# Attention in steps of two blocks, gates over the whole array, and another order in the last stripe of a hybrid decoder step

## The chip, the core and the metric

The kernel runs on one core of a Trainium2 chip. A core has a matrix engine (TensorE, PE in the profile, with its weight loads as PEld), a vector engine (VectorE, DVE), an engine for activation functions (ScalarE, ACT), a general engine (GpSimd, POOL) and an engine that here only issues DMAs (SyncE, SP). Each works through its own queue in order, and semaphores tie them together. Matmuls write to PSUM, eight banks of 512 floats in each of 128 partitions; everything else lies in SBUF. The metric is the device time of one execution in microseconds (us), lower is better.

## What is computed

One layer of a hybrid decoder: 1024 prompt tokens and 8 sample tokens, one after the other branch, in fp32. The parts that the change touches are the gates of the recurrence (16 blocks of 64 channels, two 64x64 matrices each), the blocked attention (3 groups of 8 heads, 8 query blocks of 128, each against one or two key blocks) and the output projection with its norm:

```python
def rg_lru(xc, h0, w_a, b_a, w_x, b_x, lam):
    xb = xc.reshape(B, T, N_RNN_BLOCKS, RNN_BLOCK)
    r = sigmoid(einsum('btnc,ncd->btnd', xb, w_a) + b_a)
    i = sigmoid(einsum('btnc,ncd->btnd', xb, w_x) + b_x)
    ...
def dilated_attention_prompt(q, k, v, window, dilation, slopes):
    ...
    s = jnp.where(mask, einsum('brnqhe,brnkhe->brnhqk', qb, kc) * HEAD_DIM ** -0.5 + bias, NEG_INF)
    lse = logsumexp(s, axis=-1)
    o = einsum('brnhqk,brnkhe->brnqhe', exp(s - lse[..., None]), vc)
def hybrid_layer(...):
    proj = rms_norm(x, norm_pre) @ w_in
    u, z_rnn, q, k, v, z_attn, g_rnn, g_attn = split(proj)
    ...
    mixed = sigmoid(g_rnn) * y_rnn + sigmoid(g_attn) * y_attn
    return x + rms_norm(mixed @ w_out, norm_post)
```

## The kernel before

**Products.** Every large product is made of three fp32r products, since operands are split into a high and a low part (`xh`, `xl`; `whi`, `wlo`): high x high, high x low, low x high, all accumulated in one PSUM tile with the tag `pj`. `project` makes a 128-column matrix in three chunks of tokens (256, 384 and 392 wide, 24 matmuls each); an `evac` on ACT or DVE then takes the chunk out of PSUM. There are 3 `pj` tiles, 3 `s` tiles, 1 `pt` and 1 `o`: all eight banks.

**Order.** All code is recorded in the order in which it is written, and each engine keeps that order. The projections run one after another: `u` and `z` of the recurrence, `za`, six gate matrices `g`, then for each of four head pairs `hp` and three groups `g` the matrices v, k and q, then the other `g`. Everything else is in generators on lanes ("lru", "attention", "merge", "sample"). After every half chunk (12 matmuls) `tick` lets each lane that is due make one step; what a generator yields is how many planned nanoseconds of PE work later its next step is due. When the arena of SBUF slots (`NSLOT` of them) is empty, `Arena.get` calls `force`, which runs the next due lane steps at once, with no projection work between them, until a slot is free.

**Gates.** `chain(j)` takes the channel blocks 2j and 2j+1 through convolution, gates and scan; `chain_front` holds the gate products. For each half `s` of 64 channels and each chunk, the high weights `lh` multiply the tile `xs[s]` (its one half of the partitions holds the high part of the input, the other half the low part) over all 128 rows, and the low weights `ll` multiply the 64 rows with the high part only. The result goes to an `s` tile, from which two sigmoids on ACT (L591) take it. All three chunks are one lane step.

**Attention.** `attention(g, hp)` has 12 steps. Step b does `turn(b - 2)` (transposes of the probabilities into `pt`, copied to `PT`), `scores(b)` (one matmul per head, 64 rows each, into an `s` tile of its own; a fused add and minimum on DVE, L802; the exponential on ACT, L806), and `values(b - 4)` (64 output columns per head, four blocks in one `o` tile). Steps also hold `v_rows` and `k_rows`, which transpose v and k.

**Last stripe.** The output projection is made in four stripes of 256 columns; in each, blocks 0 to 7 of the prompt and then block 8 (the 8 sample rows) are multiplied (`out_block`). In the last stripe `finish` closes blocks in groups, after blocks 2, 4, 6 and 8: reciprocal root on DVE and ACT, scale and residual, store. For blocks in `SHARED` one half of the columns goes through ACT and POOL.

Of the kernel before, what the change touches and what calls it, by code (L numbers as in the profile page):

```python
# [29 lines left out]
NSLOT = 43  # L30
# [3 lines left out]
LAG, STEP = 2, 1700  # L34
# [35 lines left out]
def hybrid_step(ctx: ExitStack, tc: tile.TileContext, I, O):  # L70
# [10 lines left out]
    def ps_tile(tag):  # L81
        bufs = {"pj": 3, "s": 3, "pt": 1, "o": 1}[tag]
        return psum.tile([128, 512], F32, tag=tag, bufs=bufs, name="ps_" + tag)
# [468 lines left out]

    def chain_front(b, X, R, T):
# [27 lines left out]
        for s in range(2):  # L581
            rows = slice(64 * s, 64 * s + 64)
            ws = slice(128 * s, 128 * s + 128)
            for c0, n in CHUNKS:
                p = ps_tile("s")
                cs = slice(c0, c0 + n)
                mm(p[:, :n], lh[:, ws], xs[s][:, cs], start=True, stop=False)
                mm(p[:, :n], ll[rows, ws], xs[s][rows, cs], start=False, stop=True)
                for gate in range(2):
                    at = 64 * (gate ^ s)  # L590
                    nc.scalar.activation(G[gate][rows, cs], p[at:at + 64, :n], AF.Sigmoid,  # L591
                                         bias=par[rows, b, 5 + gate:6 + gate])
            yield 1500
# [184 lines left out]
    def attention(g, hp):  # L778
# [14 lines left out]
        def scores(b):  # L793
            k0, n = keys(b)
            pt = P[b] = small.tile([128, 2, 256], F32, tag="P", name="P", bufs=LAG + 1)
            base = C["base2"] if g == 2 else C["base0"][:, 256 - 128 * n:256]
            for h in range(2):
                p = ps_tile("s")
                hs = slice(64 * h, 64 * h + 64)
                mm(p[:, :128 * n], qt[hs, 128 * b:128 * b + 128], kt[hs, 128 * k0:128 * (k0 + n)],  # L800
                                 start=True, stop=True)
                nc.vector.tensor_tensor_reduce(out=pt[:, h, :128 * n], in0=p[:, :128 * n], in1=base,  # L802
                                               scale=-SLOPES[g][2 * hp + h] * DIL[g], scalar=3e38,
                                               op0=OP.add, op1=OP.min, accum_out=st[:, g, 0, h, b:b + 1])
            for h in range(2):
                nc.scalar.activation(pt[:, h, :128 * n], pt[:, h, :128 * n], AF.Exp, scale=-1.0,  # L806
                                     bias=st[:, g, 0, h, b:b + 1], accum_out=st[:, g, 1, h, b:b + 1])

        def turn(b):
            k0, n = keys(b)  # L810
            pt = P.pop(b)
            p = ps_tile("pt")
            for h in range(2):
                for kb in range(n):
                    tr(p[:, (h * n + kb) * 128:(h * n + kb) * 128 + 128],
                                        pt[:, h, 128 * kb:128 * kb + 128], ident)
            t = PT[b] = small.tile([128, 2 * n, 128], F32, tag="PT", name="PT", bufs=LAG + 1)
            src = p[:, :256 * n].rearrange("p (b c) -> p b c", c=128)
            if b % 2:
                nc.vector.tensor_copy(t, src)  # L820
            else:
                nc.scalar.activation(t, src, AF.Copy)

        def values(b):
            k0, n = keys(b)
            vn = vns[g, hp]
            t = PT.pop(b)
            if b % 4 == 0:
                PO[0] = ps_tile("o")
            o = PO[0]  # L830
            off = 128 * (b % 4)
            for kb in range(n):
                for h in range(2):
                    mm(o[64 * h:64 * h + 64, off:off + 128], vn[:, k0 + kb, 64 * h:64 * h + 64],
                                     t[:, h * n + kb], start=kb == 0, stop=kb == n - 1)
            if b % 4 == 3:
                f = b // 4
# [10 lines left out]
        for b in range(8 + 2 * LAG):  # L848
            if LAG <= b < 8 + LAG:
                turn(b - LAG)  # L850
            if b < 8:
                scores(b)
            if b >= 2 * LAG:
                values(b - 2 * LAG)
            if b < 2:
                v_rows(g, hp, b)
            elif 6 <= b < 8:
                k_rows(g, hp, b - 6)
            if b == 7:
                ar.free(kts.pop((g, hp)), qts.pop((g, hp)))  # L860
            if b == 7 + 2 * LAG:
# [304 lines left out]
    for e in started:  # L1166
        advance(e)
    C = late_consts()
# [122 lines left out]
    SHARED = (5, 6, 7)  # L1291
    ends = {2: (0, 1, 2), 4: (3, 4), 6: (5, 6), 8: (7, 8)}

    def finish(tbs):
# [4 lines left out]
        for q, tb in enumerate(tbs):  # L1299
# [3 lines left out]
            own = slice(0, 512 if tb in SHARED else D)  # L1303
            nc.vector.scalar_tensor_tensor(o[:m, own], o[:m, own], r[:m, q:q + 1], x[:m, own], op0=OP.mult, op1=OP.add)
            nc.sync.dma_start(dst[:, own], o[:m, own])
# [41 lines left out]
    order = range(9)  # L1347
    for s in range(4):
        wts = [W.use(), W.use(2)]
# [38 lines left out]
```

## Time and profile before

| | before |
|---|---|
| median of three runs | 1315.66 us (1314.17 to 1316.99) |
| the profiled execution, its own time | 1316.49 us |
| its span, first to last instruction | 1314.1 us |
| PE busy | 1294.3 us (98%) |
| PEld busy | 1203.1 us (92%) |
| DVE busy | 604.8 us (46%) |
| ACT busy | 550.0 us (42%) |
| POOL busy | 219.8 us (17%) |
| PE's share of the chain that ended last | 94% |

How to read it: a group of the table of lines gives busy time, count and mean duration, but matmuls are pipelined, so a matmul's duration says little about its cost. What a matmul costs PE is the distance from its start to the start of the next one, and that is read from the timeline. The timeline gives start, duration, engine, line, operation, tiles and shapes; `64*128` is rows times columns of the loaded weights, `x4` means that four instructions of one kind were merged into one row. An fp32 matmul (scores, values) leaves two records, an fp32r matmul and a transpose one.

### The profile page before, as it was taken

The page shows a single profiled execution, that of the slowest core. Times are in us where ns is not written, and L with a number is a line of the kernel's source. Part 1 is how long each engine was busy: PE and PEld are TensorE (multiplying, and loading weights), DVE is VectorE, ACT ScalarE, POOL GpSimd, SP SyncE. Part 2 cuts the span into 40 slices and gives each one's busy share as a digit, 9 for nine tenths or more (in the row PEclk, how much of TensorE's full clock was granted, in tenths as well). Part 3 has the DMA queues.
Part 4 walks back from the last instruction along what each step waited for, and adds up shares of the span by engine and source line. Part 5 has one row for each costly group of instructions (what it writes and reads, how often), then busy time and mean ns, then how long its engine had stood idle before and what let it go on. Part 6 is the DMA issues. An engine that isn't in the chain of part 4 may idle for free.

```text
span 1314.1 us, 21425 instructions
## 1 busy us (share of the span) xinstructions
PE 1294.3 (98%) x8726; PEld 1203.1 (92%) x8726; DVE 604.8 (46%) x1300; ACT 550.0 (42%) x1223; POOL 219.8 (17%) x228
## 2 busy tenths in 40 slices
PE   8999999999999999999999999999999999999996
PEld 8998999989998898888988988888989999999996
DVE  6552744827436324533345325544244245555225
ACT  6548357384574343334334333333563222122222
POOL 4001402314022002240016002140026000001001
PEclk9999999999999999999999999999999999999998
DMA  7201300423302017312354115421285356313033
GB/s 237 69 23 33 98 16 17 145 81 131 95 17 89 25 41 206 87 51 65 89 137 102 41 41 169 109 66 45 50 228 158 120 184 211 105 65 98 32 113 146
DMA packets 149303, 125.96 MB, mean 96 GB/s; under 512 B 8857, under 2 KB 135289, under 8 KB 149198
## 3 DMA queue, kind: packets, MB, share of 16 engines
q1 hardware_dynamic: 149206, 124.61, 31.6%
q8 instruction: 68, 1.11, 0.4%
q14 instruction: 29, 0.24, 0.1%
HBM read 98.44 MB, written 26.21 MB: 95 GB/s over the span
## 4 chain that ended last, share of the span: by engine, by line
PE 94%; DVE 2%; ACT 1%; issue 1%; DMA 0%; POOLq 0%; POOL 0%; SPq 0%; ACTq 0%; DVEq 0%
PE ps_pj L146 79%; PE ps_s L146 7%; PE ps_o L146 3%; PE ps_s L150 3%; PE ps_pt L150 2%; DVE ck L1036 1%; ACT P L806 0%; DMA wraw<-in_w_in 0%; DVE wlo L226 0%; DVE tanh L631 0%; ACT whi L225 0%; DVE PT L820 0%; DVE P L802 0%; POOLq L1384 0%; ACT whi L243 0%
## 5 line engine op out<-in xcount | busy, mean ns | idle before, releaser
L146 PE MATMUL ps_pj<-xh,whi 128*128 128x256 f32 (+3 forms) x1760 | 579.1, 329 | 0.0
L146 PE MATMUL ps_pj<-xh,wlo 128*128 128x256 f32 (+3 forms) x1760 | 558.1, 317 | 0.3 <-DVE wlo L239 0.3
L146 PE MATMUL ps_pj<-xl,whi 128*128 128x256 f32 (+3 forms) x1760 | 558.0, 317 | 0.0
L146 PEld LDWEIGHTS ps_pj<-xh,whi 128*128 128x128 f32 x1760 | 331.6, 188 | 22.8 <-issue 20.9
L146 PEld LDWEIGHTS ps_pj<-xl,whi 128*128 128x128 f32 x1760 | 331.8, 189 | 0.2
L146 PEld LDWEIGHTS ps_pj<-xh,wlo 128*128 128x128 f32 x1760 | 331.4, 188 | 0.5 <-DVE wlo L239 0.5
L226 DVE TENSOR_TENSOR wlo<-wraw,whi 128x512 fp32r<-128x512 f32 x176 | 152.5, 867 | 296.3 <-ACT whi L225 285.9
L806 ACT ACTIVATE P<-P,stat 128x128 f32<-128x128 f32 (+1 forms) x192 | 85.0, 443 | 123.9 <-DVE stat L802 123.8
L225 ACT ACTIVATE whi<-wraw 128x512 fp32r<-128x512 f32 x176 | 109.4, 623 | 7.6 <-DVE tanh L632 3.0
L146 PE MATMUL ps_pj<-wlo,mh 128*128 128x256 f32 (+1 forms) x288 | 79.1, 281 | 0.0
L146 PE MATMUL ps_pj<-whi,ml 128*128 128x256 f32 x256 | 72.0, 281 | 0.0
L146 PE MATMUL ps_pj<-whi,mh 128*128 128x256 f32 x256 | 72.0, 281 | 0.0
L802 DVE CUSTOM_DVE_ANT_0 P<-ps_s,base 128x128 f32<-128x128 f32 (+1 forms) x192 | 59.7, 347 | 21.6 <-PE ps_s L146 18.2
L820 DVE COPY PT<-ps_pt 128x512 f32<-128x512 f32 (+1 forms) x48 | 28.8, 600 | 87.8 <-PE ps_pt L150 49.9
L706 ACT ACTIVATE qt<-ps_pj,qsc 128x384 f32<-128x384 f32 (+1 forms) x36 | 27.4, 762 | 94.8 <-PE ps_pj L146 94.8
L146 PE MATMUL ps_s<-kt,qt 64*128 64x128 f32 (+1 forms) x384 | 59.0, 372 | 3.2 <-DVE stat L802 3.2
L146 PE MATMUL ps_pj<-hzl,whi 128*128 128x256 f32 (+2 forms) x192 | 61.5, 320 | 0.0
L146 PE MATMUL ps_pj<-hzh,wlo 128*128 128x256 f32 (+2 forms) x192 | 61.5, 320 | 0.0
L146 PE MATMUL ps_pj<-hzh,whi 128*128 128x256 f32 (+2 forms) x192 | 61.4, 320 | 0.0
L1088 ACT ACTIVATE sg<-ps_pj 128x256 f32<-128x256 f32 (+2 forms) x48 | 21.9, 457 | 92.8 <-PE ps_pj L146 90.8
L591 ACT ACTIVATE gate<-ps_s,par 64x256 f32<-64x256 f32 (+2 forms) x96 | 52.1, 542 | 13.2 <-PE ps_s L146 10.5
L146 PE MATMUL ps_o<-PT,vn 128*64 128x128 f32 x560 | 52.2, 292 | 1.3 <-ACT ot L846 1.3
(243 smaller groups left out, 1679.2 us busy)
## 6 DMA issues: line engine op xcount, KB each, us to landing
wraw<-in_w_in SPq DMA_DIRECT2D x72, 512.0 KB
ck<-in_cache_kv_w SPq DMA_DIRECT2D x24, 512.0 KB
sgd<-sg SPq DMA_DIRECT2D x16, 516.0 KB
sgl<-sgd SPq DMA_DIRECT2D x16, 516.0 KB
xin<-in_x_prompt SPq DMA_DIRECT2D x16, 512.0 KB
qb<-sd SPq DMA_DIRECT2D x12, 512.0 KB
fb<-fd SPq DMA_DIRECT2D x24, 256.0 KB
hzd<-uc SPq DMA_DIRECT2D x8, 516.0 KB
```

The source lines that it names most:

```text
L146: nc.tensor.matmul(out, lhsT, rhs, start=start, stop=stop)
L150: nc.tensor.transpose(out, in_, idn)
L225: nc.scalar.activation(hi[:, a:b], raw[:, a:b], AF.Copy)
L226: nc.vector.tensor_tensor(lo[:, a:b], raw[:, a:b], f32(hi[:, a:b]), op=OP.subtract)
L591: nc.scalar.activation(G[gate][rows, cs], p[at:at + 64, :n], AF.Sigmoid, bias=par[rows, b, 5 + gate:6 + gate])
L706: nc.scalar.activation(dst, src, AF.Copy, scale=C["qsc"][:, g, hp:hp + 1])
L802: nc.vector.tensor_tensor_reduce(out=pt[:, h, :128 * n], in0=p[:, :128 * n], in1=base, scale=-SLOPES[g][2 * hp + h] * DIL[g], scalar=3e38, ...
L806: nc.scalar.activation(pt[:, h, :128 * n], pt[:, h, :128 * n], AF.Exp, scale=-1.0, bias=st[:, g, 0, h, b:b + 1], accum_out=st[:, g, 1, h, ...
L820: nc.vector.tensor_copy(t, src)
L1036: nc.vector.tensor_tensor(acc, acc, t, op=OP.add)
L1088: nc.scalar.activation(z[:, c0:c0 + n], p[:, :n], AF.Sigmoid)
```

## The change

Five edits, none of which changes what is computed.

1. PSUM: `pj` goes from 3 tiles to 2, `pt` from 1 to 2. The arena loses one slot.
2. Gates: the low weights lie in two fixed tiles `low_w` of which the quarters that must not count are zero (cleared once on POOL), so that the second product also runs over all 128 rows. Only the two quarters that matter are subtracted on DVE. The lane now yields after every chunk, 1300 planned ns, in place of after three chunks, 1500.
3. Attention: a step takes two blocks. `turn`, `scores` and `values` get a pair; there are 6 steps, due 3400 planned ns apart in place of 1700. The scores of one head of both blocks share one `s` tile.
4. Last stripe: the sample rows (block 8) come first, block 7 last; `finish` runs after 8, 1, 3, 5, 6 and 7.
5. `SHARED` is now 4, 5, 6; block 7 is finished in two column halves on DVE, each stored as soon as it is done.

```diff
-NSLOT = 43
+NSLOT = 42
-LAG, STEP = 2, 1700
+STEP = 3400
...
-        bufs = {"pj": 3, "s": 3, "pt": 1, "o": 1}[tag]
+        bufs = {"pj": 2, "s": 3, "pt": 2, "o": 1}[tag]
...
+    low_w = [const.tile([128, 256], F32R, name=f"low_w{i}") for i in range(2)]
+
+    def clear_low_w():
+        for t in low_w:
+            for q in range(2):
+                nc.gpsimd.tensor_scalar(t[:, 128 * q:128 * q + 128], ident, 0.0, None, op0=OP.mult)
...
-        ll = small.tile([128, 256], F32R, tag="t2", name="ll")
+        ll = low_w[b % 2]
         nc.scalar.activation(lh, lw, AF.Copy)
-        nc.vector.tensor_tensor(ll, lw, f32(lh), op=OP.subtract)
+        for s in range(2):
+            rows, ws = slice(64 * s, 64 * s + 64), slice(128 * s, 128 * s + 128)
+            nc.vector.tensor_tensor(ll[rows, ws], lw[rows, ws], f32(lh[rows, ws]), op=OP.subtract)
...
                 mm(p[:, :n], lh[:, ws], xs[s][:, cs], start=True, stop=False)
-                mm(p[:, :n], ll[rows, ws], xs[s][rows, cs], start=False, stop=True)
+                mm(p[:, :n], ll[:, ws], xs[s][:, cs], start=False, stop=True)
...
-            yield 1500
+                yield 1300
...
+        def scores(bs):
+
+            ps = [ps_tile("s") for _ in range(2)]
+            for b in bs:
+                k0, n = keys(b)
+                off = 256 * (b % 2)
+                for h in range(2):
+                    hs = slice(64 * h, 64 * h + 64)
+                    mm(ps[h][:, off:off + 128 * n], qt[hs, 128 * b:128 * b + 128], kt[hs, 128 * k0:128 * (k0 + n)],
+                       start=True, stop=True)
...
-        for b in range(8 + 2 * LAG):
-            if LAG <= b < 8 + LAG:
-                turn(b - LAG)
-            if b < 8:
-                scores(b)
-            if b >= 2 * LAG:
-                values(b - 2 * LAG)
...
+        pairs = [(2 * i, 2 * i + 1) for i in range(4)]
+        for i in range(6):
+            if 1 <= i < 5:
+                turn(pairs[i - 1])
+            if i < 4:
+                scores(pairs[i])
+            if i >= 2:
+                values(pairs[i - 2])
+            if i < 2:
+                v_rows(g, hp, i)
+            elif i < 4:
+                k_rows(g, hp, i - 2)
...
-    SHARED = (5, 6, 7)
-    ends = {2: (0, 1, 2), 4: (3, 4), 6: (5, 6), 8: (7, 8)}
+    SHARED = (4, 5, 6)
+    ends = {8: (8,), 1: (0, 1), 3: (2, 3), 5: (4, 5), 6: (6,), 7: (7,)}
...
+            parts = [slice(0, 512)] if tb in SHARED else [slice(0, 512), slice(512, D)] if tb == 7 else [slice(0, D)]
...
-    order = range(9)
     for s in range(4):
+
+        order = list(range(9)) if s < 3 else [8] + list(range(8))
```

Three places show how the instructions stand. The first is PE's queue at a gate step of channel blocks 2 and 3. Before, one step holds three chunks (`uc` is the tile `xs[s]`):

```order
L146 MATMUL ps_pj<-xh_20_119,wlo_1942 128x392
L146 MATMUL ps_s<-uc_118_2018,lh 128x256
L146 MATMUL ps_s<-uc_118_2018,ll 128x256
L146 MATMUL ps_s<-uc_118_2018,lh 128x384
L146 MATMUL ps_s<-uc_118_2018,ll 128x384
L146 MATMUL ps_s<-uc_118_2018,lh 128x392
L146 MATMUL ps_s<-uc_118_2018,ll 128x392
L146 MATMUL ps_pj<-xh_21_120,whi_1941 128x392
```

Now most chunks stand alone between half chunks of a projection, but the last eight of these two channel blocks stand in a row, between the last chunk of `z` of block 7 and the first of `za` (the next free slot of the arena was wanted there):

```order
L146 MATMUL ps_pj<-xh_24_123,wlo_2125 128x392
L146 MATMUL ps_s<-uc_120_2090,lh 128x392
L146 MATMUL ps_s<-uc_120_2090,low_w_135 128x392
L146 MATMUL ps_s<-uc_125_2174,lh 128x392
L146 MATMUL ps_s<-uc_125_2174,low_w_136 128x392
L146 MATMUL ps_s<-uc_121_2091,lh 128x256
L146 MATMUL ps_s<-uc_121_2091,low_w_135 128x256
L146 MATMUL ps_s<-uc_126_2175,lh 128x256
L146 MATMUL ps_s<-uc_126_2175,low_w_136 128x256
L146 MATMUL ps_s<-uc_121_2091,lh 128x384
L146 MATMUL ps_s<-uc_121_2091,low_w_135 128x384
L146 MATMUL ps_s<-uc_126_2175,lh 128x384
```

What moved: six matmuls of one step became six steps of two, except for this run of sixteen (twelve rows shown are its beginning), which no projection work divides.

The second place is PE's queue in the attention of head pair 1, group 0. Before, two steps of one block each, with twelve projection matmuls between them:

```order
L146 MATMUL ps_pj<-xh_24_123,wlo_5227 128x256
L150 MATMUL ps_pt<-ident,P 128x128 x4
L146 MATMUL ps_s<-kt_4919,qt_5095 128x256 x2
L146 MATMUL ps_o<-PT,vn_5264 64x128 x4
...
L146 MATMUL ps_pj<-xh_20_119,wlo_5227 128x384
L150 MATMUL ps_pt<-ident,P 128x128 x4
L146 MATMUL ps_s<-kt_4919,qt_5095 128x256 x2
L146 MATMUL ps_o<-PT,vn_5264 64x128 x4
```

Now one step of two blocks:

```order
L146 MATMUL ps_pj<-xl_28_127,whi_5216 128x384
L146 MATMUL ps_pj<-xh_20_119,wlo_5217 128x384
L150 MATMUL ps_pt<-ident,P 128x128 x8
L146 MATMUL ps_s<-kt_4926,qt_5075 128x256 x4
L146 MATMUL ps_o<-PT,vn_5253 64x128 x8
L146 MATMUL ps_pj<-xh_21_120,whi_5216 128x384
```

What moved: the instructions are the same, but transposes, scores and values of two blocks stand together, and 24 or 36 projection matmuls stand between two steps.

The third place is ACT's queue in the first attention call (head pair 0, group 0). Before, all gates of blocks 6 and 7 stood ahead of it, and one table load preceded its exponentials:

```order
L617 ACTIVATE sq_3773<-tanh_3692 128x1032
L706 ACTIVATE qt_3723<-ps_pj,qsc 128x384 x2
L708 ACTIVATE smp<-ps_pj 128x8
L225 ACTIVATE whi_3818<-wraw_3600 128x512
L806 ACT_TABLE_LOAD
L806 ACTIVATE P,stat<-P,stat 128x128 x2
```

Now the sigmoids of those gates stand between the exponentials, each change with a table load:

```order
L823 ACT_TABLE_LOAD
L823 ACTIVATE P,stat<-P,stat 128x128 x2
L823 ACTIVATE P,stat<-P,stat 128x256 x2
L601 ACT_TABLE_LOAD
L601 ACTIVATE gate_3803<-ps_s,par 64x256
L601 ACTIVATE gate_3804<-ps_s,par 64x256
L225 ACTIVATE whi_3746<-wraw_3542 128x512
L601 ACTIVATE gate_3825<-ps_s,par 64x256
L601 ACTIVATE gate_3826<-ps_s,par 64x256
L840 ACTIVATE PT<-ps_pt 128x256
L823 ACT_TABLE_LOAD
L823 ACTIVATE P,stat<-P,stat 128x256 x4
```

What moved: the last part of the recurrence (blocks 6 and 7) now runs beside the first attention calls; ACT's queue has 37 table loads where it had 31.

## Rows read from the trace of the kernel before

**Rows 1.** The page's table of engines: busy us (share of the span) and instructions.
```profile
PE 1294.3 (98%) x8726; PEld 1203.1 (92%) x8726; DVE 604.8 (46%) x1300; ACT 550.0 (42%) x1223; POOL 219.8 (17%) x228
```

**Rows 2.** Timeline of PE around one gate step: start us, duration us, engine, line, tiles.
```profile
186.37 0.34 PE L146 MATMUL ps_pj<-xh,wlo 128*128 128x384 f32 x1
186.55 0.28 PE L146 MATMUL ps_s<-uc,lh 128*128 128x256 f32 x1
186.76 0.38 PE L146 MATMUL ps_s<-uc,ll 64*128 64x256 f32 x1
187.07 0.44 PE L146 MATMUL ps_s<-uc,lh 128*128 128x384 f32 x1
...
188.54 0.44 PE L146 MATMUL ps_pj<-xh,whi 128*128 128x392 f32 x1
188.83 0.34 PE L146 MATMUL ps_pj<-xl,whi 128*128 128x392 f32 x1
189.01 0.34 PE L146 MATMUL ps_pj<-xh,wlo 128*128 128x392 f32 x1
```

**Rows 3.** Table of PE's groups by shape: count, busy us, mean ns.
```profile
L146 PE MATMUL ps_s<-uc,lh 128*128 128x256 f32 x16 | 4.5, 279 | 0.0
```

**Rows 4.** Timeline of PE in the attention of head pair 0, group 1.
```profile
552.43 0.44 PE L146 MATMUL ps_o<-PT,vn 128*64 128x128 f32 x4
552.80 0.39 PE L146 MATMUL ps_pj<-xh,whi 128*128 128x256 f32 x1
...
555.63 0.28 PE L146 MATMUL ps_pj<-xh,wlo 128*128 128x256 f32 x1
555.75 0.60 PE L150 MATMUL ps_pt<-ident,P 128*128 128x128 f32 x4
556.28 0.70 PE L146 MATMUL ps_s<-kt,qt 64*128 64x256 f32 x4
556.91 0.66 PE L146 MATMUL ps_o<-PT,vn 128*64 128x128 f32 x8
557.50 0.44 PE L146 MATMUL ps_pj<-xh,whi 128*128 128x384 f32 x1
557.78 0.34 PE L146 MATMUL ps_pj<-xl,whi 128*128 128x384 f32 x1
```

**Rows 5.** Timeline of PE as a chunk of the third za matrix starts.
```profile
251.65 0.34 PE L146 MATMUL ps_pj<-xh,whi 128*128 128x392 f32 x1
```

**Rows 6.** Timeline of ACT: first half of the evacuation of the chunk two before it.
```profile
252.74 0.36 ACT L676 ACTIVATE za<-ps_pj 128x256 f32<-128x256 f32 x1
```

**Rows 7.** Timeline of DVE: the second half of that evacuation.
```profile
255.46 0.42 DVE L677 TENSOR_TENSOR za<-ps_pj,za 128x256 f32<-128x256 f32 x1
```

**Rows 8.** Timeline of ACT: the six sigmoids of one gate step.
```profile
200.64 3.31 ACT L591 ACTIVATE gate<-ps_s,par 64x256 f32<-64x256 f32 x6
```

**Rows 9.** Waits of PE: us in total, times, longest us.
```profile
PE ps_s L146 <- DVE stat L802: 3.2, 3, 1.9
PE ps_o L146 <- ACT ot L846: 1.3, 1, 1.3
PE ps_pt L150 <- DVE PT L820: 1.2, 1, 1.2
```

**Rows 10.** Stretches: length, busy us of PE, PEld, DVE, ACT, POOL, PE clock, DMA.
```profile
864.00:866.00 2.00, 0.53 (x3) 0.49 (x4) 2.00 (x7) 0.49 (x2) 1.94 (x1) 0.99 0.00 0
866.00:869.40 3.40, 3.40 (x16) 2.42 (x15) 2.46 (x6) 2.67 (x10) 3.32 (x2) 0.50 0.38 108
```

**Rows 11.** The page's groups: exponentials and table loads on ACT in attention.
```profile
L806 ACT ACTIVATE P<-P,stat 128x128 f32<-128x128 f32 (+1 forms) x192 | 85.0, 443 | 123.9 <-DVE stat L802 123.8
...
L806 ACT ACT_TABLE_LOAD x6 | 7.7, 1283 | 2.7 <-DVE stat L802 2.6
```

**Rows 12.** Timeline of all engines at the end of the span.
```profile
1303.80 0.28 PE L146 MATMUL ps_pj<-whi,mhl 128*72 128x256 f32 x1
...
1305.92 0.14 DVE L1297 TENSOR_REDUCE sst<-ssq 128x2 f32<-128x8 f32 x1
...
1307.53 1.94 DVE L1304 SCALAR_TENSOR_TENSOR on<-on,rstd,xin 128x512 f32<-128x512 f32 x2
...
1311.04 0.30 SPq L1305 DMA_DIRECT2D out_y_s<-on  x1
```

More of the change, by code (lines that the diff above doesn't have):

```diff
@@ L791, in keys @@
             return (b, 1)
[L793 to L813, printed above, removed]
-                for kb in range(n):
[L815 to L837, printed above, removed]
+        def scores(bs):
[7 more added lines that the diff above has]
+                       start=True, stop=True)
+            for b in bs:
+                k0, n = keys(b)
+                off = 256 * (b % 2)
+                pt = P[b] = small.tile([128, 2, 256], F32, tag="P", name="P", bufs=2)
+                base = C["base2"] if g == 2 else C["base0"][:, 256 - 128 * n:256]
+                for h in range(2):
+                    nc.vector.tensor_tensor_reduce(out=pt[:, h, :128 * n], in0=ps[h][:, off:off + 128 * n], in1=base,
+                                                   scale=-SLOPES[g][2 * hp + h] * DIL[g], scalar=3e38,
+                                                   op0=OP.add, op1=OP.min, accum_out=st[:, g, 0, h, b:b + 1])
+                for h in range(2):
+                    nc.scalar.activation(pt[:, h, :128 * n], pt[:, h, :128 * n], AF.Exp, scale=-1.0,
+                                         bias=st[:, g, 0, h, b:b + 1], accum_out=st[:, g, 1, h, b:b + 1])
@@ new lines, in turn @@
+        def turn(bs):
+            for b in bs:
+                k0, n = keys(b)
+                pt = P.pop(b)
+                p = ps_tile("pt")
+                for h in range(2):
+                    for kb in range(n):
+                        tr(p[:, (h * n + kb) * 128:(h * n + kb) * 128 + 128],
+                           pt[:, h, 128 * kb:128 * kb + 128], ident)
+                t = PT[b] = small.tile([128, 2 * n, 128], F32, tag="PT", name="PT", bufs=4)
+                src = p[:, :256 * n].rearrange("p (b c) -> p b c", c=128)
+                if b % 2:
+                    nc.vector.tensor_copy(t, src)
+                else:
+                    nc.scalar.activation(t, src, AF.Copy)
@@ new lines, in values @@
+        def values(bs):
+            vn = vns[g, hp]
+            for b in bs:
+                k0, n = keys(b)
+                t = PT.pop(b)
+                if b % 4 == 0:
+                    PO[0] = ps_tile("o")
+                o = PO[0]
+                off = 128 * (b % 4)
+                for kb in range(n):
+                    for h in range(2):
+                        mm(o[64 * h:64 * h + 64, off:off + 128], vn[:, k0 + kb, 64 * h:64 * h + 64],
+                           t[:, h * n + kb], start=kb == 0, stop=kb == n - 1)
+            if bs[-1] % 4 == 3:
+                f = bs[-1] // 4
+                o = PO[0]
@@ L846, in values @@
                 nc.scalar.activation(dst, src, AF.Copy)
-        for b in range(8 + 2 * LAG):
-            if LAG <= b < 8 + LAG:
-                turn(b - LAG)
-            if b < 8:
-                scores(b)
-            if b >= 2 * LAG:
-                values(b - 2 * LAG)
[L855 to L859, printed above, removed]
+        pairs = [(2 * i, 2 * i + 1) for i in range(4)]
[10 more added lines that the diff above has]
+                k_rows(g, hp, i - 2)
+            if i == 3:
                 ar.free(kts.pop((g, hp)), qts.pop((g, hp)))
-            if b == 7 + 2 * LAG:
+            if i == 5:
                 ar.free(vns.pop((g, hp)))
@@ L1167, in hybrid_step @@
         advance(e)
+    clear_low_w()
     C = late_consts()
@@ L1302, in finish @@
             dst = O["y_p"][0, tb * 128:(tb + 1) * 128] if tb < 8 else O["y_s"].rearrange("b o d -> (b o) d")
-            own = slice(0, 512 if tb in SHARED else D)
-            nc.vector.scalar_tensor_tensor(o[:m, own], o[:m, own], r[:m, q:q + 1], x[:m, own], op0=OP.mult, op1=OP.add)
-            nc.sync.dma_start(dst[:, own], o[:m, own])
+            parts = [slice(0, 512)] if tb in SHARED else [slice(0, 512), slice(512, D)] if tb == 7 else [slice(0, D)]
+            for own in parts:
+                nc.vector.scalar_tensor_tensor(o[:m, own], o[:m, own], r[:m, q:q + 1], x[:m, own],
+                                               op0=OP.mult, op1=OP.add)
+                nc.sync.dma_start(dst[:, own], o[:m, own])
             if tb in SHARED:
```

## The prediction

> **What bounds the kernel now.** I read the table of engines first: PE is busy in 98% of the span, DVE in 46%, ACT in 42% [rows 1]. So time is gained only where PE's queue gets shorter or stops waiting, and lost only where it waits. But a busy PE isn't a PE at its pace. I therefore went on to PE's timeline and took distances from start to start. Inside a projection a 256-column matmul costs 0.12 us (555.63 to 555.75 [rows 4]), a 384-column one 0.18 us (186.37 to 186.55), a 392-column one 0.18 us (188.83 to 189.01 [rows 2]). Where PE goes from 128-row weights to 64 rows or 64 columns, or back, it costs more, and the whole change is about the number of such places. Then I read the waits of PE: those in attention make 5.7 us [rows 9], so there is little waiting left to take away. Last I read when PSUM tiles come free, since edit 1 takes one from the projections.
>
> **Gates over the whole array.** In the gate step of rows 2 the 256-column product with 128 rows (`lh`) starts at 186.55 and the 64-row one (`ll`) at 186.76, 0.21 us in place of 0.12; `ll` lasts to 187.07, 0.31 us in place of 0.12. From 186.55 to 188.83, when the first projection matmul behind the step is through, it is 2.28 us. At the projection's pace the same seven matmuls are 2 x (0.12 + 0.18 + 0.18) + 0.18 = 1.14 us. With zeros in the unused quarters all of them are 128x128 fp32r matmuls like those of the projection, so I take the whole difference, 1.14 us, and there are 16 such steps [rows 3]: **-18.2 us**. That the chunks now stand alone costs nothing by this price, as no shape changes. DVE subtracts a quarter as many elements in two instructions; the cover is DVE's idle half.
>
> A rule of the Trainium skill speaks against this edit: "TensorE: Matmul & The Clock Gate", section "Why this matters for your kernels", says a matmul with few rows takes as long as one with all of them, and gains only from running beside others. By it full rows would give nothing here, and the sum would be 18.2 us higher. The row differs: `ll` took 0.31 us where a 256-column matmul takes 0.12 [rows 2, 4].
>
> **Attention in pairs.** A full step (transposes, scores, values) runs from 555.75 to 557.50, 1.75 us, and the first projection matmul behind it takes 0.28 us (557.50 to 557.78), 0.10 more than usual. In a pair, what does the second block save? The way into the 64-row shape: 0.09 us (0.21 less 0.12 in rows 2). The way back: 0.10 us. Of the values: two matmuls (four records) took 0.37 us (552.43 to 552.80), four took 0.59 us (556.91 to 557.50) [rows 4]; so a matmul is 0.11 us and 0.15 us is the way in and out. For scores and transposes I take no gain, each passes at its price. Twelve steps become six: the two merges without values save 0.09 + 0.10 = 0.19 us each, the four with values 0.34 us. That is 1.74 us a call, and 12 calls make **-20.9 us**. Bounds: 0.10 us a merge (only the way back), 7 us in all, to 25 us if the scores' second pair also overlaps. I stay at 20.9, since each part is a row.
>
> **The end.** PE's last matmul starts at 1303.80 and is through at 1304.08; the span ends 10.0 us later [rows 1, 12], and the last store is issued at 1311.04, 7.0 us behind PE, held up in SP's queue by the half block that went through ACT and POOL. Now block 7 is last and is finished on DVE alone. By the same rows, shifted, ACT is first at block 6's scaling till about 0.6 us behind PE (an estimate); square and product take 0.9 us more; from the reduce to the scaling it is 1.61 us (1305.92 to 1307.53); two halves of 512 columns take 1.4 us (1.94 us for one of 512 and one of 1024 columns, so 0.7 for 512). The last store is issued some 4.6 us behind PE: 2.4 us earlier, but it is a larger one. **-2.1 us** (-1.5 to -2.6). Between ends the groups of at most two blocks keep DVE free in time for two PSUM tiles.
>
> **Waits that go.** Scores waited for `s` tiles (3.2 us), values for `o` (1.3), transposes for the single `pt` (1.2) [rows 9]; pairs with 24 matmuls between them and a second `pt` tile give each more time. Behind the longest one (PE busy 0.53 of 2.00 us) the clock was granted at 0.50, that is 1.2 GHz, for 3.40 us, in which 16 matmuls passed [rows 10]; that costs half, 1.7 us. Of 7.4 us in all I count half gone, since DVE's long sample instructions stay: **-3.7 us** (0 to -7.4).
>
> **Two `pj` tiles.** The chunk that starts at 251.65 [rows 5] would now need the tile whose evacuation ACT does at 252.74 [rows 6] and DVE ends at 255.46 + 0.42 = 255.88 [rows 7]: 4.2 us late. DVE and ACT are then in the recurrence's burst of long instructions, which runs at its own pace, so PE, once it has waited, is behind that burst and doesn't wait the same time again. I take 4.2 us once and 0.5 us for smaller cases: **+4.7 us** (1, if the burst falls elsewhere, to 9, if it happens at two of them).
>
> **Sixteen gate matmuls in a row.** At the end of `z` of block 7, eight chunks now stand in PE's queue with three `s` tiles. Each needs two sigmoids, 3.31 / 6 = 0.55 us each [rows 8]. The eighth chunk starts when the sigmoids of the fifth are done: 0.3 + 10 x 0.55 + 0.36 to its end = 6.2 us, against 2.6 us of PE work. **+3.5 us** (2 to 6, the latter if all 8.8 us of ACT show).
>
> **The recurrence beside the first attention.** The gates of blocks 6 and 7 now fall between the exponentials of the first call: six more table loads, 1283 ns each [rows 11], 7.7 us of ACT in some 25 us. In a step ACT then has four exponentials (4 x 0.44), two loads (2.6) and two to four sigmoids (1.1 to 2.2), 5.5 to 6.6 us, against a period of about 24 x 0.18 + 3 = 7.3 us of PE. It fits narrowly: **+2 us** (0 to 8). Small excursions of sample and merge that now stand alone: **+0.5 us**. Clearing `low_w` on POOL, one slot less: nothing, weight pieces stand in the same order on ACT.
>
> **Sum.** -18.2 - 20.9 - 2.1 - 3.7 + 4.7 + 3.5 + 2 + 0.5 = -34.2 us. The profiled execution took 1316.49 us, which gives 1282.3; it lies 0.8 us over the median of 1315.66, so the forecast is **1281.5 us**.
>
> **The rivals.** (a) The 64-row matmul isn't slow for its shape but for its operands (`xs` is rewritten just before); then full rows give nothing: 1281.5 + 18.2 = 1299.7. For it: the `lh` products between them are slow as well (187.07 onward). Against it: the first `lh`, on the same operands, takes the usual 279 ns [rows 3] and the step to `ll` starts the loss. Chance 0.07.
> (b) The clock. In the run of sixteen and in the waits for `pj` PE is busy less than half of the time, as it was before the 3.40 us at 1.2 GHz [rows 10]. Three such falls at 1.7 us, and 3 us more of waiting for ACT: 1281.5 + 8 = 1289.5. Chance 0.15. The Trainium skill has this: "TensorE: Matmul & The Clock Gate", section "A second HAM failure mode: psum-queue depth-cycling", says that short PE pauses at PSUM tiles bring the clock down again and again. By it each such place here pays 1.7 us more; rows 9 show three waits of over 1 us, and rows 10 a fall behind one.
> (c) Slower: a turn now needs the four exponentials of the step just before, not of two steps before. Four reduces and four exponentials end about 2.5 us behind the scores; the cover is 24 matmuls and the values, some 5 us. If ACT and DVE have over 2.5 us of other work queued ahead of them in every step, PE waits in all 48 turns (4 in each of 12 calls). It decides at 34.2 / 48 = 0.7 us a turn; at 1 us the time is 1281.5 + 48 = 1329.5. Against it: ACT is busy 42%, and its own idle time ahead of exponentials, 123.9 us, is waiting for DVE's result [rows 11], not work. Chance 0.03.
> (d) The order shows that pairs and full rows are really there; that an edit does nothing can be left out for these.
>
> **How the numbers follow.** The forecast has 0.75, (a) 0.07, (b) 0.15, (c) 0.03. The forecast's own range from its terms, not all at their ends together, is 1271 to 1293; (b) lies inside it. (a) and (c), 0.10, are left out above, and about 0.08 of the rest on both sides. So 1271 to 1295. A measurement of this kernel can tell 0.2% (2.6 us) from no change. All cases but (c) are faster: 0.96 faster, 0.01 same, 0.03 slower.
>
> **What would show it.** In the profile after: the distance from `lh` to `low_w` and from `low_w` onward at 0.12 to 0.18 us; 72 attention steps, a full pair near 3.2 us; waits of PE for `pj` behind ACT or DVE between 200 and 260 us; a stretch of some 6 us with eight gate chunks; the last store some 4.6 us behind PE. It is wrong if PE's own distances don't shrink, or if waits at turns and tiles sum to over 20 us.

## The result and the profile after

The changed kernel takes 1293.1 us (median; 1290.8 to 1295.5), against 1315.3 us before: ratio 0.983, 95% interval 0.981 to 0.985. That is 22.2 us faster; the forecast was 34.2. The time lies within the range, 1.9 us below its upper end, nearer to the 1289.5 of rival (b) than to the forecast. The profiled execution took 1294.3 us with a span of 1292.5.

The page's table of engines after, to be held against [rows 1], and the view of cores (span, mean granted clock):

```profile
PE 1258.5 (97%) x8726; PEld 1209.8 (94%) x8726; DVE 604.6 (47%) x1323; ACT 553.2 (43%) x1231; POOL 221.9 (17%) x232
```
```profile
core 0: 1292.5 us, clock 0.987
```

PE's busy time fell by 36 us, the span by 22 only. So PE now has 34 us without work where it had 20, and its mean clock is 0.987 where the profile before has 0.996. **The work shrank more than forecast, and much of that was given back as waits and as clock.** First the work. Timeline of PE after, around one gate chunk:

```profile
103.93 0.28 PE L146 MATMUL ps_s<-uc,lh 128*128 128x256 f32 x1
104.05 0.28 PE L146 MATMUL ps_s<-uc,low_w 128*128 128x256 f32 x1
104.17 0.34 PE L146 MATMUL ps_pj<-xh,whi 128*128 128x392 f32 x1
```

From start to start, `lh` and `low_w` cost 0.12 us each, where [rows 2] had 0.21 and 0.31. And a full pair in group 0 (transposes, scores, values, then the first projection matmuls behind them):

```profile
559.70 1.03 PE L150 MATMUL ps_pt<-ident,P 128*128 128x128 f32 x8
560.66 1.14 PE L146 MATMUL ps_s<-kt,qt 64*128 64x256 f32 x8
561.73 1.09 PE L146 MATMUL ps_o<-PT,vn 128*64 128x128 f32 x16
562.75 0.44 PE L146 MATMUL ps_pj<-xh,whi 128*128 128x384 f32 x1
563.03 0.34 PE L146 MATMUL ps_pj<-xl,whi 128*128 128x384 f32 x1
```

Against two of the steps of [rows 4] (0.53 + 0.63 + 0.59, and 0.10 on the way back): transposes 0.96 for 1.06, scores 1.07 for 1.26, values 1.02 for 1.18, one way back for two. That is 0.55 us a pair. Over the 12 calls, added up from start to start and with the transposes of v and k that stand there, attention's places cost about 136 us of PE in place of 168.

Now what came back. Waits of PE after (us in total, times, longest):

```profile
PE ps_pj L146 <- DVE za L687: 11.0, 5, 4.9
PE ps_s L146 <- ACT gate L601: 2.7, 5, 0.7
PE ps_pj L146 <- ACT whi L225: 2.7, 1, 2.7
PE ps_pt L150 <- ACT P L823: 2.3, 2, 2.2
```

The three waits of [rows 9] are gone; these four took their place, 18.7 us for 5.7. And the clock: stretches of the kernel after (length, busy us of PE, PEld, DVE, ACT, POOL, PE clock, DMA share, GB/s):

```profile
11.80:15.20 3.40, 3.01 (x14) 3.02 (x15) 2.08 (x5) 1.64 (x5) 2.83 (x8) 0.51 1.11 375
220.00:223.40 3.40, 3.40 (x18) 3.40 (x17) 0.00 (x0) 3.27 (x6) 1.78 (x1) 0.50 0.00 0
243.90:250.70 6.80, 3.88 (x12) 3.88 (x13) 6.70 (x5) 0.00 (x0) 2.79 (x2) 0.50 0.00 0
264.30:267.70 3.40, 3.35 (x10) 3.35 (x11) 3.32 (x6) 0.00 (x0) 0.00 (x0) 0.51 0.35 103
458.90:462.30 3.40, 3.40 (x23) 2.57 (x20) 1.79 (x10) 2.36 (x9) 2.31 (x1) 0.50 0.02 5
...
1182.50:1189.30 6.80, 6.30 (x28) 6.01 (x29) 2.41 (x4) 1.82 (x5) 0.00 (x0) 0.50 0.90 303
sum 30.60, PE 26.74 PEld 25.57 DVE 17.36 ACT 9.10 POOL 9.72; mean PE 3.82 PEld 3.65 DVE 2.48 ACT 1.30 POOL 1.39
```

PE worked 26.7 us at 1.2 GHz (clock 0.50); half of it, 13 us, would not be there at 2.4 GHz. Before there was one such stretch ahead of PE's end [rows 10], 1.7 us. The first of the seven, 1.5 us of the 13, lies in the kernel's start; the profile of e10, whose start is that of the kernel before, has one there too (12.1 to 15.5 us), so it isn't to be put down to the change. Ahead of most of the others stands one of the waits, with PE busy for 0.1 to 0.6 of the time:

```profile
213.00:220.00 7.00, 4.32 (x21) 2.95 (x20) 0.57 (x1) 6.57 (x13) 0.00 (x0) 1.00 0.26 75
261.00:264.30 3.30, 0.52 (x3) 0.20 (x2) 2.97 (x4) 2.89 (x6) 0.00 (x0) 1.00 0.80 320
1180.00:1182.50 2.50, 0.20 (x2) 0.00 (x0) 0.57 (x1) 0.86 (x2) 0.74 (x3) 1.00 0.69 213
```

### The profile page after: what moved, and what is told of

Read it like the earlier page. It is cut to its first block, busy times and chain, and to the rows that moved or that the text cites. A ratio compares the mean times of both kernels' runs of the same rounds, so it can differ in the third digit from the quotient of the medians.

```text
span 1292.5 us, 21498 instructions
## 1 busy us (share of the span) xinstructions
PE 1258.5 (97%) x8726; PEld 1209.8 (94%) x8726; DVE 604.6 (47%) x1323; ACT 553.2 (43%) x1231; POOL 221.9 (17%) x232
## 4 chain that ended last, share of the span: by engine, by line
PE 87%; ACT 5%; DVE 5%; issue 1%; DMA 1%; POOL 0%; SPq 0%; DVEq 0%; ACTq 0%
PE ps_pj L146 75%; PE ps_s L146 5%; PE ps_o L146 3%; PE ps_s L150 3%; PE ps_pt L150 2%; ACT gate L601 1%; DVE wlo L226 1%; DVE tanh L641 1%; ACT whi L225 1%; DMA wraw<-in_w_in 1%; DVE ck L1057 1%; ACT gate L623 1%; ACT sq L627 0%; ACT P L823 0%; ACT L627 0%
## 5 line engine op out<-in xcount | busy, mean ns | idle before, releaser
L146 PE MATMUL ps_pj<-xh,whi 128*128 128x256 f32 (+3 forms) x1760 | 574.7, 327 | 12.1 <-DVE za L687 11.0
L146 PEld LDWEIGHTS ps_pj<-xh,whi 128*128 128x128 f32 x1760 | 334.0, 190 | 21.0 <-DVE za L687 12.4
L226 DVE TENSOR_TENSOR wlo<-wraw,whi 128x512 fp32r<-128x512 f32 x176 | 149.6, 852 | 320.0 <-ACT whi L225 314.0
L819 DVE CUSTOM_DVE_ANT_0 P<-ps_s,base 128x128 f32<-128x128 f32 (+1 forms) x192 | 56.0, 348 | 8.5 <-PE ps_s L146 8.0
L840 ACT ACTIVATE PT<-ps_pt 128x256 f32<-128x256 f32 (+1 forms) x48 | 21.0, 437 | 91.0 <-PE ps_pt L150 90.9
L146 PEld LDWEIGHTS ps_pj<-wlo,mh 128*128 128x128 f32 (+1 forms) x288 | 52.3, 181 | 0.5 <-DVE wlo L226 0.4
```

Source lines behind the costliest of these rows:

```text
L146: nc.tensor.matmul(out, lhsT, rhs, start=start, stop=stop)
L226: nc.vector.tensor_tensor(lo[:, a:b], raw[:, a:b], f32(hi[:, a:b]), op=OP.subtract)
```

## Experiments

**Theory.** Pairs and full rows are worth what PE's distances say (32 and 18.8 us); what is missing comes back by four side effects of the change: two `pj` tiles, the gates cut into single chunks ("the cut" from here on), one slot fewer, and the clock behind the waits. **Rivals.** One of the two large edits gives less than its distances; the `za` waits come from one side effect alone; the late weights have nothing to do with the slot.

The diffs are against the kernel before (e1 to e4, e10, e12) or after (e5 to e9, e11). The kernel before took 1314.7 to 1315.5 us beside them.

### e1 and e12: pairs alone

```diff
+        pairs = [(2 * i, 2 * i + 1) for i in range(4)]
+        for i in range(6):
+            if 1 <= i < 5:
+                turn(pairs[i - 1][:1])
+            if i < 4:
+                scores(pairs[i])
+            if i >= 2:
+                values(pairs[i - 2])
+            if 1 <= i < 5:
+                turn(pairs[i - 1][1:])
...
```

> The kernel before with attention in pairs alone; PSUM stays at three pj tiles and one pt tile, so the second block's transposes stand behind the values and have the pt tile to themselves. Theory: the work in PE's queue shrinks by what the trace after shows for pairs, 136.3 us in place of 168.2 in the 12 calls, -32 us, less a little for the extra place with transposes: 1283 to 1288 us. Rival (the prediction's price): the second pair of scores costs a full pass and what is beyond 20.9 us came with the second pt tile: 1294 to 1297 us. Rival (turns wait): the exponentials of the step just before come late in most steps: above 1300 us.

Measured: 1277.3 us, ratio 0.971 (0.968 to 0.973): **-38.2 us**, more than any side expected. This one edit alone beats the whole change. PE has no wait over 0.4 us left in attention and no half clock there. So to the 32 us of work come the 5.7 us of waits and the 1.7 us of clock of [rows 9, 10], which the expectation had left out: 39.4. The prediction's price for a merge was too small.

e12 is the same with both `turn`s ahead of the scores, as the change has it, and with `"pj": 2` and `"pt": 2`:

> The kernel before with attention in pairs exactly as the change writes them (both blocks turned one behind the other) and with its two pj and two pt tiles; gates, slots and last stripe as before. To be held against the two tiles alone (1324.4 us). Theory: pairs are worth as much in this form as in the form with three pj tiles (-38 us): 1284 to 1289 us. Rival: the split transposes gave part of it, and as written pairs are worth the prediction's 20.9 us and 5.7 us of waits: 1296 to 1300 us.

Measured: 1288.3 us, ratio 0.980 (0.977 to 0.982), 36.1 us below the two tiles alone (e3). Pairs are worth nearly the same in both forms (38.2 and 36.1). It also says that pairs and tiles by themselves give 26.9 us: **all the rest of the change together cost 4.9 us.**

### e2: full-row gates alone

```diff
+        ll = low_w[b % 2]
...
-                mm(p[:, :n], ll[rows, ws], xs[s][rows, cs], start=False, stop=True)
+                mm(p[:, :n], ll[:, ws], xs[s][:, cs], start=False, stop=True)
```

> The kernel before with full-row gates alone, three chunks in a step as before; the zeroed weights live in one of the 43 slots until the last gate. Theory: sixteen steps lose 1.17 us each, -18.8 us and nothing else: 1295 to 1298 us. Rival: the 64-row product is slow for its operands and full rows give nothing: 1314 to 1316 us. Rival: full rows give 18.8 us, but a part comes back as waits even without the cut into chunks: 1299 to 1306 us.

Measured: 1303.2 us, ratio 0.990 (0.987 to 0.992): -12.4 us, the last of the three. Full rows do give, which ends rival (a) of the prediction. But of the 18.8 us of work a third comes back. Waits of PE in e2 and two stretches of it (columns as above):

```profile
PE ps_s L146 <- ACT gate L602: 3.6, 6, 0.9
```
```profile
190.00:196.60 6.60, 4.54 (x23) 3.36 (x21) 0.00 (x0) 6.39 (x13) 0.00 (x0) 1.00 0.00 0
196.60:200.00 3.40, 3.21 (x14) 3.21 (x15) 0.00 (x0) 3.29 (x7) 2.39 (x1) 0.50 0.00 0
```

PE is now faster than ACT's sigmoids (0.55 us each, two to a chunk [rows 8]) and there are three `s` tiles; ACT is busy in 6.39 of 6.60 us, PE waits, and the clock falls behind it. Before, with the slow 64-row product between the chunks, the profile has no such wait. Whether more tiles help is e11.

### e3: two `pj` and two `pt` tiles alone

```diff
-        bufs = {"pj": 3, "s": 3, "pt": 1, "o": 1}[tag]
+        bufs = {"pj": 2, "s": 3, "pt": 2, "o": 1}[tag]
```

> The kernel before with two pj tiles and two pt tiles, nothing else. Theory: PE's waits for pj tiles in the za projections (237 to 278 us) come from the two tiles alone: some 12 us of waiting and 3 to 7 us of half clock behind it, less 1 us for the second pt tile: 1326 to 1334 us, with PE waiting for DVE's za. Rival: those waits come from the gates cut into chunks, which push the recurrence's long instructions onto za; then two tiles alone cost what the prediction said or less: 1316 to 1321 us.

Measured: 1324.4 us, ratio 1.006 (1.004 to 1.008): +8.8 us, between the two. Its waits of PE:

```profile
PE ps_pj L146 <- DVE zs L550: 2.4, 3, 2.0
...
PE ps_pj L146 <- DVE za L677: 2.2, 3, 1.0
...
PE ps_pj L146 <- DVE on L1341: 1.5, 1, 1.5
```

6.1 us of waiting, at three kinds of chunk, and one half-clock stretch behind the kernel's start (219.3 to 222.8 us). But on `za` 2.2 us, where the kernel after has 11.0: the tiles alone don't explain those.

### e5, e6 and e7: the tiles or the cut set back in the kernel after

e5 sets the tiles back (`"pj": 3`, `"pt": 1`) and nothing else:

> The kernel after (1293.1 us) with three pj tiles and one pt tile. Theory: the 12 us of waiting for pj and some 4 us of half clock go, but each pair now turns two blocks through one pt tile, and the second waits for the first one's evacuation (0.44 us on ACT and the way to it): 48 waits of 0.5 to 0.9 us, 24 to 43 us: 1300 to 1320 us. Rival: the scores queued on ACT and DVE let that evacuation through at once and the wait is hidden: 1277 to 1283 us.

Measured: 1327.9 us, ratio 1.009 (1.006 to 1.012), above the range of the theory, with its mechanism:

```profile
PE ps_pt L150 <- ACT PT L840: 35.9, 48, 3.8
```

Every pair waits for the evacuation between its two blocks, 0.75 us on average. So the second `pt` tile belongs to pairs that are written in this way; the tile is paid for at `pj`. e6 takes the three tiles and is meant to avoid that wait: the second block turns behind the values.

```diff
-                turn(pairs[i - 1])
+                turn(pairs[i - 1][:1])
...
+            if 1 <= i < 5:
+                turn(pairs[i - 1][1:])
```

> The kernel after with three pj tiles and one pt tile, and the second block's transposes behind the values. Theory: waits for pj and their half clock go (some 16 us), pairs keep their gain, one more place with transposes costs up to 5 us: 1277 to 1284 us. Rival: the waits come from the gates in chunks and not from the tiles: 1291 to 1296 us.

Measured: 1287.7 us, ratio 0.979 (0.978 to 0.981): -5.5 us against after, and neither side is right. Its three largest waits of PE:

```profile
PE ps_pt L150 <- ACT PT L840: 7.2, 4, 2.8
PE ps_pj L146 <- DVE za L687: 4.5, 2, 3.4
PE ps_pj L146 <- DVE wlo L226: 3.4, 2, 3.0
```

With a third tile PE gets further at `za`, and then waits for the next thing that DVE owes it, the low half of the weights. The largest wait, for the single `pt` tile, is not gone: in three of the four cases (387 to 447 us, the first attention calls) the evacuation of `pt` stands on ACT behind sigmoids of the gates or the recurrence's other work, which the cut has put beside attention; e9, without the cut, has 0.9 us of such waiting. So what a third `pj` tile is worth for itself, e6 doesn't show. e7 leaves the two tiles and takes the gates in steps of three chunks again:

```diff
-                yield 1300
+            yield 1500
```

> The kernel after with three chunks of the gates in a step, as before the change; two pj tiles stay. Theory: the run of sixteen gate matmuls with its 4 us of waiting and the half clock behind it go, and no gates are left beside attention: -5 to -9 us, 1284 to 1288 us, with PE's waits for DVE's za still there (8 us or more). Rival (chunks cause the za waits): those go as well: 1272 to 1279 us.

Measured: 1281.4 us, ratio 0.975 (0.973 to 0.976): -11.7 us, between the two; the waits for `za` fall from 11.0 to 2.6 us, those for `zs` are 2.2. So the two causes stand side by side: PE's waits for DVE, at `pj` and the low weights, are 11 us with both, 8 with the cut alone (e6), 5 to 6 with two tiles alone (e3, e7), none to speak of with neither (e9). The kernel after shows why the cut does it. PE waits 4.9 us as a chunk starts; then ACT, all sixteen sigmoids of the run in one row; then DVE:

```profile
246.82 0.69 PE L146 MATMUL ps_pj<-xh,whi 128*128 128x392 f32 x1 [4.94 <-DVE za L687]
```
```profile
213.62 9.13 ACT L601 ACTIVATE gate<-ps_s,par 64x392 f32<-64x392 f32 x16
...
237.17 0.38 ACT L686 ACTIVATE za<-ps_pj 128x256 f32<-128x256 f32 x1
```
```profile
225.53 1.42 DVE L226 TENSOR_TENSOR wlo<-wraw,whi 128x512 fp32r<-128x512 f32 x1 [11.21 <-ACT whi L225]
...
237.27 1.22 DVE L631 SCALAR_TENSOR_TENSOR tanh<-gate,tanh 128x1032 f32<-128x1032 f32 x1
...
241.75 2.74 DVE L633 TENSOR_SCALAR gate<-tanh 128x1032 f32<-128x1032 f32 x1
244.59 1.23 DVE L635 SCALAR_TENSOR_TENSOR sq<-gate,sq 128x1032 f32<-128x1032 f32 x1
246.35 0.42 DVE L687 TENSOR_TENSOR za<-ps_pj,za 128x256 f32<-128x256 f32 x1
246.68 4.13 DVE L641 TENSOR_TENSOR_SCAN tanh<-gate,sq 128x1024 f32<-128x1024 f32 x1
```

DVE idles 11.2 us while ACT works off the run, and later gets the recurrence's long instructions in one block. A `za` chunk that ACT had taken at 237.17 has its product on DVE at 246.35, 9.2 us later; at 246.82 PE may go on, after 4.9 us.

### e4 and e8: the slot

e4 is the kernel before with `NSLOT = 42`, the number of slots in the arena; e8 is the kernel after with 43, in which `low_w` is an arena tile that is freed after the last gate:

```diff
+        low_t = new([128, 2, 256], F32R, "low_w")
...
+        if b == 7:
+            ar.free(low_w[2])
```

> The kernel before with 42 slots in place of 43, nothing else. Theory: the output projection's first weights are then asked for one step later, PE waits for ACT's whi about 2.7 us at the start of that stage and the clock is granted at 0.50 behind it: 1318 to 1322 us. Rival: that wait in the kernel after has nothing to do with the slot (it comes from the work ahead of it having become shorter): 1314 to 1316.5 us.

> The kernel after with 43 slots; the zeroed gate weights live in one of them until the last gate and it is free from then on. Theory: the wait for whi at 1182 us (2.7 us) and the half clock behind it (3.4 us of PE time in 6.8 us) go: -4 to -6 us, 1287 to 1289.5 us. Rival: the wait stays, 1292 to 1294 us.

Measured: e4 1322.1 us, ratio 1.004 (1.002 to 1.005), **+6.6 us**, with 2.6 us of waiting for `whi` and half clock from 1208.4 to 1211.8; e8 1282.8 us, ratio 0.976 (0.974 to 0.979), **-10.3 us** against after, more than either side expected, without that wait. The wait for `whi` is shown from both sides. The whole size isn't: the profiled execution of e4 took 1318.0 us; eight of its nine others have a mean clock of 0.991 to 0.993 where the profiled one has 0.997, and no trace shows where they lost it. Before, then after, at the start of the output projection (all engines; SPq is the issue of the load):

```profile
1194.18 0.38 SPq L207 DMA_DIRECT2D wraw<-in_w_out  x1
...
1203.02 0.62 ACT L225 ACTIVATE whi<-wraw 128x512 fp32r<-128x512 f32 x1
...
1205.51 0.28 PE L146 MATMUL ps_pj<-whi,mh 128*128 128x256 f32 x1
```
```profile
1178.62 4.57 SPq L207 DMA_DIRECT2D wraw<-in_w_out  x5
...
1182.17 1.15 ACT L225 ACTIVATE whi<-wraw 128x512 fp32r<-128x512 f32 x2 [1.63 <-DMA wraw<-in_w_out]
...
1182.85 0.58 PE L146 MATMUL ps_pj<-whi,mh 128*128 128x256 f32 x1 [2.66 <-ACT whi L225]
```

Before, the second half of the first stripe's weights is split 2.5 us ahead of the stage. After, no slot is free for it during the last block of the stage ahead, so it is asked for when the stage begins, and PE stops after four of the eight k steps. From the stage's first matmul to PE's last it takes 98.3 us in the trace of before, 104.6 after and 98.3 in e8. The other 4 us of e8's gain lie ahead of it; 3 of them are clock (PE works 6 us less at 1.2 GHz there than after), and what sets that is open (see the end).

### e10: the last stripe alone

Its edits are 4 and 5 of the change.

> The kernel before with the last stripe's order and finishing alone. Theory (from the trace after): the span's end stands 9.0 us behind PE's last matmul in place of 10.0 us: -1 us, 1313 to 1315 us. Rival (the prediction): -2.1 us, 8 us behind PE's last matmul, 1312 to 1314 us. Rival: the edit costs, since smaller groups wait on DVE in the middle of the stripe: 1316 us or more.

Measured: 1314.8 us, ratio 0.999 (0.998 to 1.000): too small to be told from nothing. In its profile the span ends 9.0 us behind PE's last matmul, as in the kernel after, in place of 10.0.

### e9 and e11: the parts that pay, joined

e9 is the kernel after with e6, e7 and e8 together. e11 also sends the gates' chunks round five tiles:

```diff
-                p = ps_tile("s")
+                gate_n[0] += 1
+                p = ps_tile(("s", "pt", "s", "o", "s")[gate_n[0] % 5])
```

> The kernel after with four things set back or mended at once: three pj tiles and one pt tile with the second block's transposes behind the values, three chunks of the gates in a step, and 43 slots with the zeroed gate weights in one of them until the last gate. Pairs, full-row gates and the end of the last stripe stay. Theory: the three edits' gains add once the waits are gone: -38.2 us (pairs alone), -12.4 us (gates alone), -1 us (end) from 1315.3: 1261 to 1267 us, with no wait of PE for pj tiles over 1 us and none for whi. Rival: the gains collide, since attention begins sooner behind the recurrence's last instructions: 1268 to 1275 us.

> The joined kernel with the gates' chunks going round five PSUM tiles (three s, the pt and the o tile, which nothing else uses at that time) in place of three. Theory: what full-row gates alone fell short of 18.8 us is PE waiting for s tiles until ACT's sigmoids are done (3.6 us) and a half-clock stretch behind it (1.7 us); with five tiles most of it goes: 3 to 5 us below the joined kernel. Rival: ACT's sigmoids set the pace whatever the tiles are, and the wait only moves: within 1.5 us of the joined kernel.

Measured: e9 1268.0 us, ratio 0.964 (0.962 to 0.965), at the edge between the two ranges; the single gains (38.2, 12.4, and 0.2 for the end) add up but for some 4 us. e11 **1263.6 us, ratio 0.961 (0.960 to 0.963)**, 4.4 us below e9, as the theory had it. In the stretch in which e2 waited, e9 and then e11 show

```profile
190.00:200.00 10.00, 7.74 (x39) 6.56 (x38) 0.00 (x0) 9.68 (x18) 3.20 (x2) 0.83 0.00 0
190.00:200.00 10.00, 9.06 (x59) 8.64 (x58) 0.00 (x0) 9.72 (x18) 4.62 (x2) 1.00 0.00 0
```

With three tiles PE is busy in 7.74 of 10 us at a mean clock of 0.83, with five in 9.06 at full clock, and ACT is as full in both (9.68 and 9.72): the tiles let PE do other work while ACT catches up. e11 is the fastest of all, 29.6 us below the kernel after.

## Why the prediction was right, and where it was short

Right: the sign, the range, what bounds the kernel, and the mechanism of both large edits. That the time fell inside the range is in part luck, since two errors cancelled. With the change's own tiles pairs gave 36.1 us (e12), where the sum had 20.9 and 3.7 of waits, 11.5 less; had they given only that, the time would have been about 1305 us, outside the range, because of costs that the sum had at nothing or too low. The steps one by one:

- **Gates, -18.2.** By PE's distances, waits left out, the gate products took 33.9 us (with the way back) and now take 15.0, -18.8. The term is right as work; as time it was -12.4 (e2). Two steps failed. One is the assumption that PE's own gain is the kernel's: with three chunks in a step as before, PE already waits for ACT's sigmoids (e2). The other is "That the chunks now stand alone costs nothing": the cut costs 11.7 us (e7). By the rule that was weighed there (the Trainium skill, "TensorE: Matmul & The Clock Gate", "Why this matters for your kernels": few rows take as long as all) full rows were to give nothing, and e2 is 12.4 us faster. Yet inside a run of one shape the traces agree with it: four more of the 64-row score records cost 0.44 us (1.07 less 0.63), 0.11 each, where a 128-row matmul of 256 columns costs 0.12. What is slow in [rows 2] is 64-row and 128-row products by turns.
- **Pairs, -20.9.** Mis-sized: about -31.9 as work. "For scores and transposes I take no gain" is the sentence that failed. A merge saved 0.55 us and not 0.34: 0.10 at the transposes and 0.10 more at the scores. Every passage that is twice as long saves a piece, not only those at the outer ends.
- **Waits that go, -3.7.** All of it went, 5.7 us and 1.7 us of clock (e1), where half was counted.
- **The end, -2.1.** Measured in the trace: -1.0; alone (e10) too small to be told from nothing. From the kernel after:

```profile
1283.21 0.28 PE L146 MATMUL ps_pj<-whi,ml 128*128 128x256 f32 x1
...
1284.77 0.72 ACT L1332 ACTIVATE on<-on,rstd 128x512 f32<-128x512 f32 x1 [1.77 <-DVE rstd L340]
...
1286.22 0.15 DVE L1319 TENSOR_REDUCE sst<-ssq 128x1 f32<-128x4 f32 x1
...
1287.86 1.41 DVE L1327 SCALAR_TENSOR_TENSOR on<-on,rstd,xin 128x512 f32<-128x512 f32 x2
```

  PE is through at 1283.49. Block 6's scaling holds ACT until 1285.49, 2.0 us behind PE, where 0.6 was estimated, since its root came late from DVE. The steps from the reduce on (1.64 and 1.41 us) are as forecast, so the last store is issued 5.8 us behind PE (1289.30) and not 4.6.
- **Two `pj` tiles, +4.7.** Alone +8.8 (e3), within the bounds of 1 to 9. In the kernel after it met the cut, and the waits for `za` made 11.0 us. "PE, once it has waited, is behind that burst and doesn't wait the same time again" failed: it waited at four of five chunks in a row (237 to 264 us; 1.9, 4.9, 1.1 and 2.8 us), because DVE's long instructions go on through them.
- **Sixteen in a row, +3.5.** Right. From the kernel after, the first of the sixteen and the first matmul behind them:

```profile
213.03 0.34 PE L146 MATMUL ps_s<-uc,lh 128*128 128x392 f32 x1
...
219.65 0.28 PE L146 MATMUL ps_pj<-xh,whi 128*128 128x256 f32 x1
```

  That is 6.6 us, where the sixteen at PE's pace take 2.6: 4.0 us, of which the table of waits has 2.7. What it does further on, to DVE's burst and so to `za`, was not seen; the cut as a whole costs 11.7 us (e7).
- **Recurrence beside attention, +2.** One wait of 2.2 us, and 1.7 us for the half clock behind it (458.9): within the bounds of 0 to 8. e7, with no gates beside attention, has no such wait.
- **One slot fewer, nothing.** Wrong: +6.6 alone (e4), 10.3 in the kernel after (e8). The reason given, that the weight pieces stand in the same order on ACT, doesn't hold at the output projection, where they stand behind the last `mh` and not among them. This term was put at nothing without any row for the output projection.
- **The clock.** Rival (b) came true, beside the forecast's mechanism and not in its place: it cost some 13 us where before it had cost 1.7, the largest thing in the trace that the sum had left out. It had counted three falls; there are seven stretches, six without the one at the kernel's start. By the second rule that was named (the Trainium skill, "TensorE: Matmul & The Clock Gate", "A second HAM failure mode: psum-queue depth-cycling") short pauses at PSUM tiles bring the clock down again and again. The trace bears this out in part: three of the seven stretches (220.0, 243.9, 264.3 us) follow waits for PSUM tiles; those at 458.9 and 1182.5 follow waits for data, and ahead of the one at 991.4 PE had waited only 0.4 us and then done sixteen one-column products in 1.8 us.

**The sum from the trace**, against before: work -18.8 and -31.9, old waits -5.7, end -1.0; new waits +18.7, clock +11 (13 less 1.7, with the 1.5 at the kernel's start). That is -27.7, against -21.6 in the spans. Of the 6 us between, 2.3 are that the four waits make 21.0 us from start to start, some 2 are waits under 0.6 us at other places, and under 1 is a later start beyond the clock's part in it; the rest isn't placed. **The sum from the runs**: pairs and tiles -26.9 (e12), full rows -12.4 (e2), cut +11.7 (e7), slot +6.6 (e4), end -0.2 (e10): -21.2, against -22.2 measured. That it closes so well is in part the choice of values: with the slot at e8's 10.3 it would be -17.5, and the cut was only measured in the kernel after. By this sum the gates as written, with their cut and the slot that their weights took, cost about 6 us in place of saving 18.

Not the cause: operands of the 64-row product (a; e2), turns that wait in every step (c; two waits, 2.3 us).

## What to carry to other kernels

An edit that makes the busiest engine's work shorter is worth its distances only where the engines behind it have room: ask per stage who evacuates, how long that takes per tile, and how many tiles there are. What a change takes away to make room (a PSUM tile, a slot, a yield) is to be priced with the same care as the gain; here these three (8.8 and 6.6 us alone, 11.7 set back in the kernel after) come to 27 us, of the 51 that the gains make alone, and e9 shows that none of them was needed. And a wait of the matrix engine is to be priced with the slower clock that may follow it.

## What the runs showed of the hardware

- **Turns between shapes cost in both directions, and inside a passage too.** Two blocks in one place took 3.15 us where two places took 3.70. The 0.55 us come from all three kinds of matmul (0.10, 0.19 and 0.16) and the way back (0.10), with the same number of instructions.
- **The clock doesn't follow the order of the instructions alone.** In e8 PE waits at the same transposes for the same time as in the kernel after (2.13 and 2.16 us), with the same order of PE's instructions right around them. Behind it the kernel after has 1.2 GHz for 3.4 us (458.9, above). e8, in which all this comes 2.1 us earlier, has

```profile
456.80:460.20 3.40, 3.40 (x36) 2.92 (x33) 2.37 (x11) 2.39 (x9) 2.22 (x1) 1.00 0.02 5
```

  So a single wait of 2 us may or may not bring the slower clock; what tells the two apart no run here shows. It differs between executions of one kernel too: e4 took 1318.0 us at a mean clock of 0.997 and 1324.6 at 0.991, e5 1321.4 at 0.992 and 1333.2 at 0.981. The kernel after had 0.987 in all four.
